# A three-branch decoder layer on one core: an earlier start from the un-normalised input, a hoisted merge gate, and the next block's rows moved

## The chip, the cores and the metric

The kernel runs on one core of a Trainium2 chip, on core 0. The metric is the device time of one execution in microseconds: 2474.88 us, median of 3 runs (2473.91 to 2475.95).

## What is computed

One layer reads x (2048 tokens of 1024 channels), normalises each token, projects it by one large matrix, sends the columns of the projection through three token mixers, weights each mixer's lifted output by a gate, sums, projects and adds to x. Cut to its main lines:

```python
h = _rmsnorm(x, norm_w[l])
proj = h @ w_in[l]
(a_q, a_f, a_i, a_g, b_qkv, b_z, b_beta, b_a,
 c_q, c_k, c_v, c_g, gate_logits) = jnp.split(proj, split_points, axis=-1)
y_a = _hgrn2_branch(a_q, a_f, a_i, a_g, lb_all[l], norm_a[l])       # A: gated recurrence, 4 heads
y_b = _gated_deltanet_branch(b_qkv, b_z, b_beta, b_a, conv_w[l], ...)  # B: delta rule, 4 heads, chunks of 64
y_c = _swa_sink_branch(c_q, c_k, c_v, c_g, sinks[l], bias_blk)      # C: attention in a window of 128
lifted = jnp.einsum('bsnc,ncd->bsnd', ys, w_branch[l])
gates = jax.nn.sigmoid(gate_logits.reshape(Bn, S, N_BRANCHES, D_MODEL))
merged = jnp.sum(gates * lifted, axis=2)
x = x + merged @ w_out[l]
return _rmsnorm(x, final_norm)
```

The normalisation is `x * rsqrt(mean(x*x) + eps) * w`: a factor for each token and a factor for each channel. In each chunk, branch B inverts a unit triangular 64 x 64 matrix (`triangular_solve`).

## The kernel before, in words

The tokens are worked in four blocks of 512 (`block`, s = 0 to 3). Every float32 product is split: each factor is written as a high and a low part, and three matmuls (high by high, high by low, low by high) stand for one. One weight tile is 128 x 512 for the high and for the low part and serves four steps of 128 channels, so `mm_ct` (L97) issues 12 matmuls for each tile: L102, L103 and L104 are its three matmuls. They write a bank of PSUM with the tag d (ps_d, four banks). The mixers' own small matmuls write the banks c0 and c1 (ps_c, two each).

In block 0 a weight tile comes from DRAM as `wraw`; ACT makes the high part (L87), DVE the low part (L88), and the pair is stored as `kept`. The later blocks load the kept pair into one of four buffers (L83).

The start (L207 to L221): the transposed x, times the channel factor, is split into uH and uL (un-normalised), and the projections of v, beta and the like are taken from u and scaled row by row afterwards. `load_x` (L124) loads one of eight row tiles of x (L127) and squares it on ACT with a running sum (L129); `norm_rows` and `norm_scale` make the factor of each token from these sums, spread it over the partitions by matmuls of diagonals (dg from POOL at L141, matmul L143) and copy it to R (L145). `norm_h` multiplies x by R (L158) and splits into hH (ACT, L107) and hL (DVE, L108). All further projections read h. For the blocks 1 to 3 the eight `load_x`, `norm_rows` and `norm_scale` stand at the end of the block before, in the merge of branch C, and ACT issues their loads.

The merge: `gate(n, dt)` projects one tile of gate logits and takes a tanh on ACT (L360), `lift` projects the branch's output and combines; n is the branch, dt one of eight channel tiles. One gate is 24 matmuls of L102 to L104 on hH and hL, one lift is 12 on yH and yL.

Branch B, a head h: `unit_b(h)` is the first phase. It makes NT (products of keys), copies its 64 x 64 corners to NS on ACT (L581), stores them to a DRAM scratch (L582), loads the 16 x 16 diagonal blocks as L (L585), inverts these on DVE by a loop of pairs L589 and L591, stores, loads the result as XB and transposes it into X (L596). `unit_b2` is the second phase: two levels of matmul L611 (reads X and NS), four copies to yb (L615, two on ACT and two on DVE), matmul L621 and a masked copy into X (L626); then L638 and the rest, and the recurrence over chunks (L655 and after). Branch C, a unit j: `unit_c` makes logits and exponentials E, `unit_c2` transposes E (L750), copies it to PT (ACT, L752) and multiplies it by the values (L759).

The order of the instructions on each engine is fixed when the program is built. The phases are written so that the second phase of one head stands after the first phase of the next (L811 to L861), and a scheduler interleaves them. `tc.issue_after(x)` puts what it encloses behind instruction x: L611 stands behind the last matmul issued by `mm_ct` before it (`last_mm`), so whatever projections are written ahead of the call stand ahead of L611. The lines that set this order around the change are

```python
f3(yA); pb1 = unit_b(1); f0 = pb0(); merge(0, yA, range(2)); f1 = pb1(); merge(0, yA, range(2, KT))
pb2 = unit_b(2); f1(yB); pb3 = unit_b(3); pb2()(yB); c0 = unit_c(0); pb3()(yB); c1 = unit_c(1)
```

"Head one" to "head four" below are h = 0 to 3, and "head one of the recurrence" is `unit_a(0)`.

Of the kernel before, what the change touches and what calls it, by code (L numbers as in the profile page):

```python
# [11 lines left out]
F32 = mybir.dt.float32  # L12
# [3 lines left out]
AF = mybir.ActivationFunctionType  # L16
# [4 lines left out]
P = 128  # L21
# [31 lines left out]
def _trunk(tc, S, a, out):  # L53
# [40 lines left out]
    last_mm, last_act, last_ld, last_dve = [None], [None], [None], [None]  # L94

# [35 lines left out]
    def norm_rows(sq):  # L131
        rs = sb.tile([P, NT], F32, name="rsx", tag="rsx")
        G.tensor_tensor(rs, sq[:, :, 0], sq[:, :, 1], op=ALU.add)
        rsq(rs, rs, 1.0 / D, EPS)
        return rs
# [70 lines left out]
    def start(kt):  # L206
        xT0.append(load_xT(0, kt, SLOT[kt], 2))  # L207
        uH.append(sb.tile([P, TB], F32R, name="uH", tag="msum", bufs=KT + 1))
        split(uH[kt], uL[kt], xT0[kt], normw[:, kt:kt + 1])
        load_x(0, sq0, kt, SLOT[kt])  # L210

    pj0 = mm_tc(a["wtc"][0], NTC, uH, uL, each=start)
    rs0 = norm_rows(sq0)
# [110 lines left out]
    def block(s, hH, hL, last=None):  # L324
        t0 = s * TB

        def proj_ct(idx):
            p = bank()
            mm_ct(p, a["wct"][idx], hH, hL, KT)
            return p  # L330

        def gate_ct(idx):
            pg = proj_ct(idx)
            gt = sb.tile([P, TB], F32, name="gt", tag="gt")
            silu2(gt, pg)
            return gt
# [20 lines left out]
        def gate(n, dt):  # L357
            gp = proj_ct(37 + n * KT + dt)
            th = sb.tile([P, TB], F32, name="gth", tag="gth", bufs=GB)
            A.activation(th, gp, AF.Tanh, scale=0.5)  # L360
            return th
# [22 lines left out]
        def unit_a(h):  # L384
# [4 lines left out]
            pf = proj_ct(4 + h)  # L389
# [5 lines left out]
            pq = proj_ct(h)  # L395
            silu2(Q, pq)
            gt = gate_ct(8 + h)
# [422 lines left out]
        pb1 = unit_b(1)  # L820
        f0 = pb0()
        merge(0, yA, range(2))
# [6 lines left out]
        pb3 = unit_b(3)  # L829
        pb2()(yB)  # L830
# [4 lines left out]
        merge(1, yB, range(2))  # L835
# [9 lines left out]
        c3()(yC)  # L845
        if s + 1 < NSB:
            sq = sb.tile([P, NT, 2], F32, name="sqx", tag="sqx")
            with tc.issue_after(last_act[0]):
                for i in range(2 * NT):
                    load_x(s + 1, sq, i, eng=A)  # L850
            rs = norm_rows(sq)
        for dt in range(3):
            lift(2, dt, g[dt], yC)
        merge(2, yC, range(3, 6))
        if s + 1 < NSB:
            R = norm_scale(rs, last_mm[0])
        merge(2, yC, range(6, KT))
# [97 lines left out]
```

## Time and profile before

| what | value |
| --- | --- |
| device time, median of 3 runs | 2474.88 us |
| the profiled execution, device time | 2470.34 us |
| its span, first to last instruction | 2468.6 us |
| PE (matmul) busy | 2403.5 us, 97% |
| DVE busy | 1168.6 us, 47% |
| ACT busy | 866.2 us, 35% |
| POOL busy | 437.5 us, 18% |

A busy time is the sum over one engine's instructions. Matmuls are pipelined, so one that is listed with 0.39 us lets the next start 0.23 us after its own start. In a timeline row the first number is the start in us from the start of the span, the second the duration (of all its instructions, with a count behind x), and the brackets hold the idle time of that engine just ahead of it and what released it. The granted clock is given in parts of full speed, 2.4 GHz.

### The profile page before, as it was taken

The numbers are of one execution on the slowest core, as the hardware profiler recorded it, in microseconds if no ns is written. First come the engines' busy times: TensorE is split into PE (matmuls) and PEld (weight loads), VectorE is DVE, ScalarE is ACT, GpSimd is POOL, SyncE is SP. The second block draws the span as 40 slices with busy tenths as digits, with TensorE's granted clock in tenths as the row PEclk, the third lists the DMA queues.
The fourth block names the chain that finished last, engine by engine and source line by source line (L and its number), as shares of the span: only waits on it lengthen the run. The fifth ranks groups of instructions, "written<-read, shape, count | busy, mean of one in ns | idle before, by whom it ended". The sixth has DMA issues, their size and how long they took to land. (4 is left out here: it accounts for less than half of the span.)

```text
span 2468.6 us, 37448 instructions
## 1 busy us (share of the span) xinstructions
PE 2403.5 (97%) x13658; PEld 1930.1 (78%) x13658; DVE 1168.6 (47%) x3188; ACT 866.2 (35%) x2285; POOL 437.5 (18%) x821
## 2 busy tenths in 40 slices
PE   7999999999999999999999999999999999999998
PEld 7777777878877777787887868778788786877886
DVE  5667477455245626613324562652232465274311
ACT  5455355354334313414223521341322342233211
POOL 3322021112122101111112210111111221011011
PEclk9999999999999999999999999999999999999999
DMA  6756673878844445355774445435666453543564
GB/s 226 244 195 230 225 256 123 282 248 318 289 135 125 143 165 159 106 179 194 240 215 129 139 137 175 150 105 188 208 214 207 129 157 119 183 143 117 168 202 170
DMA packets 193156, 452.84 MB, mean 183 GB/s; under 512 B 52243, under 2 KB 70588, under 8 KB 192844
## 3 DMA queue, kind: packets, MB, share of 16 engines
q1 hardware_dynamic: 180812, 442.05, 54.7%
q10 hardware_dynamic: 12160, 8.39, 1.1%
q8 instruction: 108, 1.77, 0.3%
q14 instruction: 76, 0.62, 0.1%
HBM read 348.81 MB, written 103.14 MB: 183 GB/s over the span
## 5 line engine op out<-in xcount | busy, mean ns | idle before, releaser
L102 PE MATMUL ps_d<-hH,wHL 128*128 128x512 f32 x1952 | 785.0, 402 | 7.7 <-ACT hH L107 5.6
L103 PE MATMUL ps_d<-hL,wHL 128*128 128x512 f32 x1952 | 781.3, 400 | 1.3 <-DVE hL L108 1.3
L104 PE MATMUL ps_d<-hH,wHL 128*128 128x512 f32 x1952 | 779.3, 399 | 0.0
L102 PEld LDWEIGHTS ps_d<-hH,wHL 128*128 128x128 f32 x1952 | 369.0, 189 | 76.9 <-ACT hH L107 5.7
L103 PEld LDWEIGHTS ps_d<-hL,wHL 128*128 128x128 f32 x1952 | 368.7, 189 | 71.8 <-issue 2.2
L104 PEld LDWEIGHTS ps_d<-hH,wHL 128*128 128x128 f32 x1952 | 368.3, 189 | 70.4 <-issue 1.8
L88 DVE TENSOR_TENSOR wHL<-wraw,wHL 128x512 fp32r<-128x512 f32 (+1 forms) x194 | 130.0, 675 | 115.8 <-ACT wHL L87 110.8
L374 POOL TENSOR_TENSOR msum<-msum,gth 128x512 f32<-128x512 f32 x64 | 90.0, 1408 | 407.5 <-DVE gth L373 387.6
L87 ACT CAST wHL<-wraw 128x512 fp32r<-128x512 f32 (+1 forms) x194 | 113.7, 592 | 134.2 <-PE ps_d L104 87.9
L360 ACT ACTIVATE gth<-ps_d 128x512 f32<-128x512 f32 x96 | 57.4, 598 | 289.3 <-PE ps_d L104 288.2
L103 PE MATMUL ps_d<-yL,wHL 128*128 128x512 f32 x384 | 153.7, 402 | 0.0
L102 PE MATMUL ps_d<-yH,wHL 128*128 128x512 f32 x384 | 153.5, 401 | 0.0
L104 PE MATMUL ps_d<-yH,wHL 128*128 128x512 f32 x384 | 152.9, 400 | 0.0
L373 DVE SCALAR_TENSOR_TENSOR gth<-gth,ps_d 128x512 f32<-128x512 f32 x64 | 43.9, 687 | 203.9 <-PE ps_d L104 203.9
L174 PE MATMUL ps_d<-wHL,mH 128*128 128x512 f32 x256 | 99.5, 390 | 2.7 <-DMA wHL<-kept 2.7
L175 PE MATMUL ps_d<-wHL,mH 128*128 128x512 f32 x256 | 99.6, 389 | 0.0
L176 PE MATMUL ps_d<-wHL,mL 128*128 128x512 f32 x256 | 99.5, 389 | 0.0
L517 DVE SCALAR_TENSOR_TENSOR qkB<-raw,convw,qkB 128x512 f32<-128x512 f32 x96 | 71.7, 747 | 44.1 <-ACT qkB L515 42.7
L121 ACT ACTIVATE th<-ps_d 128x512 f32<-128x512 f32 x64 | 38.3, 598 | 130.2 <-PE ps_d L104 120.8
L103 PEld LDWEIGHTS ps_d<-yL,wHL 128*128 128x128 f32 x384 | 72.4, 188 | 14.6 <-issue 1.2
L102 PEld LDWEIGHTS ps_d<-yH,wHL 128*128 128x128 f32 x384 | 72.2, 188 | 14.7 <-issue 0.7
L104 PEld LDWEIGHTS ps_d<-yH,wHL 128*128 128x128 f32 x384 | 72.4, 189 | 14.1 <-issue 1.2
(280 smaller groups left out, 3758.7 us busy)
## 6 DMA issues: line engine op xcount, KB each, us to landing
wHL<-kept SPq DMA_DIRECT2D x486, 512.0 KB, 3.5
kept<-wHL SPq DMA_DIRECT2D x162, 512.0 KB, 4.0
wraw<-in_wct_dram SPq DMA_DIRECT2D x122, 256.0 KB, 3.5
wHL<-kept SPq DMA_DIRECT2D x32, 324.0 KB, 3.7
xT<-in_xT_dram SPq DMA_DIRECT2D x32, 256.0 KB, 4.8
rt<-in_x_dram SPq DMA_DIRECT2D x32, 256.0 KB, 3.9
out_dram<-rt SPq DMA_DIRECT2D x32, 256.0 KB, 3.9
wraw<-in_wb_dram SPq DMA_DIRECT2D x24, 256.0 KB, 3.8
```

What stands on the lines that cost most here:

```text
L87: A.copy(w[:, 0, :n], raw[:, :n])
L88: V.tensor_tensor(w[:, 1, :n], raw[:, :n], w[:, 0, :n].bitcast(F32), op=ALU.subtract)
L102: T.matmul(p, wh[:, ks], rh[kt], start=(kt == 0), stop=False)
L103: T.matmul(p, wh[:, ks], rl[kt], start=False, stop=False)
L104: last_mm[0] = T.matmul(p, wl[:, ks], rh[kt], start=False, stop=(kt == nk - 1)).ins
L174: T.matmul(pj[j][:, :n], lh[kt][:, js], wh, start=(kt == 0), stop=False)
L175: T.matmul(pj[j][:, :n], lh[kt][:, js], wl, start=False, stop=False)
L176: last = T.matmul(pj[j][:, :n], ll[kt][:, js], wh, start=False, stop=(kt == KT - 1)).ins
L360: A.activation(th, gp, AF.Tanh, scale=0.5)
L373: last_dve[0] = V.scalar_tensor_tensor(th, th, 1.0, lp, op0=ALU.add, op1=ALU.mult).ins
L374: G.tensor_tensor(m, m, th, op=ALU.add)
L517: V.scalar_tensor_tensor(dst, raw[:, j:j + TB], convw[:, ti, j:j + 1], dst, op0=ALU.mult, op1=ALU.add)
```

## The change

It has four parts. (1) At the start, `load_x` lags two channel tiles behind the split of u. (2) In block 0, head one of the recurrence takes its three projections from u (`raw`) and DVE multiplies each by R into a new tile `scaled`. (3) In each block the first gate of the merge of branch A is written ahead of head one's second phase, `pb0()`, and the first gate of the merge of branch B ahead of head three's, `pb2()`; their lifts stay where they were. (4) The next block's `load_x` calls move from behind unit C's last phase into the merge of branch C, behind its fourth lift and behind the fourth gate's tanh; the `norm_scale` moves one merge step later.

```diff
@@ -92,6 +92,7 @@
         return w[:, 0, :n], w[:, 1, :n]
 
     last_mm, last_act, last_ld, last_dve = [None], [None], [None], [None]
+    last_tanh = [None]
 
     def mm_ct(p, src, rh, rl, nk):
         for q in range(nk // 4):
@@ -207,9 +208,12 @@
         xT0.append(load_xT(0, kt, SLOT[kt], 2))
         uH.append(sb.tile([P, TB], F32R, name="uH", tag="msum", bufs=KT + 1))
         split(uH[kt], uL[kt], xT0[kt], normw[:, kt:kt + 1])
-        load_x(0, sq0, kt, SLOT[kt])
+        if kt > 1:
+            load_x(0, sq0, kt - 2, SLOT[kt - 2])
 
     pj0 = mm_tc(a["wtc"][0], NTC, uH, uL, each=start)
+    for i in (KT - 2, KT - 1):
+        load_x(0, sq0, i, SLOT[i])
     rs0 = norm_rows(sq0)
     marks = []
     pj1 = mm_tc(a["wtc"][1], NTC, uH, uL, tags=("d", "d", "c1", "c1"), marks=marks)
@@ -324,13 +328,18 @@
     def block(s, hH, hL, last=None):
         t0 = s * TB
 
-        def proj_ct(idx):
+        def proj_ct(idx, raw=False):
             p = bank()
-            mm_ct(p, a["wct"][idx], hH, hL, KT)
-            return p
-
-        def gate_ct(idx):
-            pg = proj_ct(idx)
+            if not raw:
+                mm_ct(p, a["wct"][idx], hH, hL, KT)
+                return p
+            mm_ct(p, a["wct"][idx], uH, uL, KT)
+            t = sb.tile([P, TB], F32, name="scaled", tag="gth", bufs=GB)
+            V.tensor_tensor(t, p, R0, op=ALU.mult)
+            return t
+
+        def gate_ct(idx, raw=False):
+            pg = proj_ct(idx, raw)
             gt = sb.tile([P, TB], F32, name="gt", tag="gt")
             silu2(gt, pg)
             return gt
@@ -357,7 +366,7 @@
         def gate(n, dt):
             gp = proj_ct(37 + n * KT + dt)
             th = sb.tile([P, TB], F32, name="gth", tag="gth", bufs=GB)
-            A.activation(th, gp, AF.Tanh, scale=0.5)
+            last_tanh[0] = A.activation(th, gp, AF.Tanh, scale=0.5).ins
             return th
 
         def lift(n, dt, th, yT):
@@ -386,15 +395,16 @@
             hs = slice(h * P, (h + 1) * P)
             qk = sb.tile([P, 2, TB], F32, name="qk", tag="qk")
             Q, K = qk[:, 0, :], qk[:, 1, :]
-            pf = proj_ct(4 + h)
+            raw = s == 0 and h == 0
+            pf = proj_ct(4 + h, raw)
             F = sb.tile([P, TB], F32, name="F", tag="w0")
             A.activation(F, pf, AF.Sigmoid)
             A.activation(K, pf, AF.Sigmoid, scale=-1.0)
             A.activation(F, F, AF.Identity, scale=omlb[:, h:h + 1], bias=lb[:, h:h + 1])
             A.activation(K, K, AF.Copy, scale=omlb[:, h:h + 1])
-            pq = proj_ct(h)
+            pq = proj_ct(h, raw)
             silu2(Q, pq)
-            gt = gate_ct(8 + h)
+            gt = gate_ct(8 + h, raw)
             prod = sb.tile([P, TB], F32, name="prod", tag="w1")
             G.tensor_tensor(prod, Q, K, op=ALU.mult)
             V.tensor_tensor(Q, Q, F, op=ALU.mult)
@@ -818,8 +828,10 @@
         pb0 = unit_b(0)
         f3(yA)
         pb1 = unit_b(1)
+        g = gate(0, 0)
         f0 = pb0()
-        merge(0, yA, range(2))
+        lift(0, 0, g, yA)
+        merge(0, yA, range(1, 2))
         f1 = pb1()
         merge(0, yA, range(2, KT))
         yB = new_y()
@@ -827,12 +839,14 @@
         pb2 = unit_b(2)
         f1(yB)
         pb3 = unit_b(3)
+        g = gate(1, 0)
         pb2()(yB)
         c0 = unit_c(0)
         pb3()(yB)
         c1 = unit_c(1)
         f0 = c0()
-        merge(1, yB, range(2))
+        lift(1, 0, g, yB)
+        merge(1, yB, range(1, 2))
         f1 = c1()
         merge(1, yB, range(2, KT))
         yC = new_y()
@@ -843,18 +857,19 @@
         c2()(yC)
         g = [gate(2, dt) for dt in range(3)]
         c3()(yC)
+        for dt in range(3):
+            lift(2, dt, g[dt], yC)
+        merge(2, yC, range(3, 4))
         if s + 1 < NSB:
             sq = sb.tile([P, NT, 2], F32, name="sqx", tag="sqx")
-            with tc.issue_after(last_act[0]):
+            with tc.issue_after(last_tanh[0]):
                 for i in range(2 * NT):
                     load_x(s + 1, sq, i, eng=A)
             rs = norm_rows(sq)
-        for dt in range(3):
-            lift(2, dt, g[dt], yC)
-        merge(2, yC, range(3, 6))
+        merge(2, yC, range(4, 7))
         if s + 1 < NSB:
             R = norm_scale(rs, last_mm[0])
-        merge(2, yC, range(6, KT))
+        merge(2, yC, range(7, KT))
         if s + 1 < NSB:
             with tc.issue_after(last_dve[0]):
                 hs = norm_h(R, lambda kt: load_xT(s + 1, kt))
```

The places where this moves instructions follow, as the program's order has them. The changed file's line numbers are higher: L102 to L108 and L127 to L158 by one, L360 and L370 by nine, L589 to L638 and L752 by ten. L338 is the new product `scaled`.

The first place is DVE at the start of block 0. Before, the last rows ahead of the normalisation and the rows up to the first work behind it:

```order
L198 TENSOR_SCALAR ba<-ps_c_297,rsx 128x8
L88 TENSOR_TENSOR wHL<-wraw,wHL 128x512
L158 TENSOR_TENSOR xT<-xT,R 128x512 x2
L108 SCALAR_TENSOR_TENSOR hL<-xT,normw,hH 128x512 x4
L158 TENSOR_TENSOR xT<-xT,R 128x512
L108 SCALAR_TENSOR_TENSOR hL<-xT,normw,hH 128x512
L158 TENSOR_TENSOR xT<-xT,R 128x512
L108 SCALAR_TENSOR_TENSOR hL<-xT,normw,hH 128x512 x3
L88 TENSOR_TENSOR wHL<-wraw,wHL 128x512
L481 TENSOR_TENSOR xa<-ba,dtb 128x16
L482 SCALAR_TENSOR_TENSOR ab<-xa 128x16
```

and now:

```order
L199 TENSOR_SCALAR ba<-ps_c_297,rsx 128x8
L159 TENSOR_TENSOR xT<-xT,R 128x512 x2
L109 SCALAR_TENSOR_TENSOR hL<-xT,normw,hH 128x512 x4
L159 TENSOR_TENSOR xT<-xT,R 128x512
L109 SCALAR_TENSOR_TENSOR hL<-xT,normw,hH 128x512
L159 TENSOR_TENSOR xT<-xT,R 128x512
L109 SCALAR_TENSOR_TENSOR hL<-xT,normw,hH 128x512 x3
L338 TENSOR_TENSOR scaled<-ps_d,R 128x512
L88 TENSOR_TENSOR wHL<-wraw,wHL 128x512 x4
L491 TENSOR_TENSOR xa<-ba,dtb 128x16
L492 SCALAR_TENSOR_TENSOR ab<-xa 128x16
```

Before, one L88 stands ahead of the normalisation (L158 and L108) and one behind it; now none of this stretch stands ahead, and the first `scaled` and four L88 stand behind it.

The second place is head one of block 1. On PE the second phase of a delta-rule head begins with L611. Before, from the last matmul of the keys' products (L562):

```order
L562 MATMUL ps_c_8416<-qkB 128x256 x2
L562 MATMUL ps_c_8423<-qkB 128x256 x2
L103 MATMUL ps_d<-hL,wHL 128x512
L104 MATMUL ps_d<-hH,wHL 128x512
L102 MATMUL ps_d<-hH,wHL 128x512
L103 MATMUL ps_d<-hL,wHL 128x512
L104 MATMUL ps_d<-hH,wHL 128x512
L611 MATMUL ps_c_8477<-X,NS 64x64 x4
L102 MATMUL ps_d<-hH,wHL 128x512
L103 MATMUL ps_d<-hL,wHL 128x512
L104 MATMUL ps_d<-hH,wHL 128x512
L102 MATMUL ps_d<-hH,wHL 128x512
```

and now the end of the stretch between the same two lines, which are L572 and L621 there:

```order
L105 MATMUL ps_d<-hH,wHL 128x512
L103 MATMUL ps_d<-hH,wHL 128x512
L104 MATMUL ps_d<-hL,wHL 128x512
L105 MATMUL ps_d<-hH,wHL 128x512
L103 MATMUL ps_d<-hH,wHL 128x512
L104 MATMUL ps_d<-hL,wHL 128x512
L105 MATMUL ps_d<-hH,wHL 128x512
L621 MATMUL ps_c_8514<-X,NS 64x64 x4
L103 MATMUL ps_d<-yH,wHL 128x512
L104 MATMUL ps_d<-yL,wHL 128x512
L105 MATMUL ps_d<-yH,wHL 128x512
L103 MATMUL ps_d<-yH,wHL 128x512
```

Before, five matmuls of `mm_ct` stand between the two lines; now 17 do, the same kind, and the lift on yH, which stood later, follows L621 at once. On DVE, the end of the same head's two levels and the start of head two's inversion (L589), before:

```order
L615 COPY yb_506<-ps_c_8477 64x2x32 x2
L626 COPY_PREDICATED X<-bmask,ps_c_8486 64x2x2x16 x4
L632 STREAM_TRANSPOSE XB<-X 64x256 x2
L615 COPY yb_506<-ps_c_8497 64x2x32 x2
L626 COPY_PREDICATED X<-bmask,ps_c_8506 64x2x32 x4
L635 STREAM_TRANSPOSE XB<-X 32x4x32 x2
L589 TENSOR_TENSOR L16t<-L_8440 32x14
L592 MEMSET L_8440 32x16
L643 COPY Y_8524<-ps_c_8517 64x256
L591 TENSOR_TENSOR L_8440<-L_8440,L16t 32x14
```

and now:

```order
L625 COPY yb_506<-ps_c_8514 64x2x32 x2
L636 COPY_PREDICATED X<-bmask,ps_c_8523 64x2x2x16 x4
L642 STREAM_TRANSPOSE XB<-X 64x256 x2
L625 COPY yb_506<-ps_c_8534 64x2x32 x2
L379 SCALAR_TENSOR_TENSOR msum<-gth,ps_d 128x512
L599 TENSOR_TENSOR L16t<-L_8446 32x14
L602 MEMSET L_8446 32x16
L636 COPY_PREDICATED X<-bmask,ps_c_8543 64x2x32
L601 TENSOR_TENSOR L_8446<-L_8446,L16t 32x14
L636 COPY_PREDICATED X<-bmask,ps_c_8543 64x2x32
L599 TENSOR_TENSOR L16t<-L_8446 32x26
L636 COPY_PREDICATED X<-bmask,ps_c_8543 64x2x32
```

The first L599 (L589 before), which reads head two's L, has moved ahead of the four masked copies L636 (L626 before) of head one's second level, and the following pairs alternate with them.

The third place is ACT at the end of block 1, around the last copies of unit C to PT. Before:

```order
L129 ACTIVATE scrp,sqx<-xs 128x512
L127 DMA xs<-in_x_dram 128x512
L360 ACTIVATE gth<-ps_d 128x512
L129 ACTIVATE scrp,sqx<-xs 128x512
L127 DMA xs<-in_x_dram 128x512
L129 ACTIVATE scrp,sqx<-xs 128x512 x2
L360 ACTIVATE gth<-ps_d 128x512
L752 COPY PT<-ps_c_11112 128x512
L752 COPY PT<-ps_c_11119 128x512
L752 COPY PT<-ps_c_11136 128x512
L752 COPY PT<-ps_c_11143 128x512
L107 ACTIVATE yH<-gt 128x512
```

and now:

```order
L762 COPY PT<-ps_c_11118 128x512
L762 COPY PT<-ps_c_11125 128x512
L762 COPY PT<-ps_c_11142 128x512
L762 COPY PT<-ps_c_11149 128x512
L108 ACTIVATE yH<-gt 128x512
L108 ACTIVATE mH<-msum 128x512 x3
L369 ACTIVATE gth<-ps_d 128x512
L128 DMA xs<-in_x_dram 128x512 x2
L130 ACTIVATE scrp,sqx<-xs 128x512
L128 DMA xs<-in_x_dram 128x512
L108 ACTIVATE mH<-msum 128x512
```

Before, the loads (L127) and squares (L129) stand ahead of the four copies to PT, between the gates' tanh; now the four copies come first, then the splits of m (L108), the fourth gate's tanh (L369), and the loads and squares behind it, with splits between.

## Rows read from the trace of the kernel before

**Rows 1.** The page, parts 1 and 5: PE, and the merge's additions.

```profile
PE 2403.5 (97%) x13658; PEld 1930.1 (78%) x13658; DVE 1168.6 (47%) x3188; ACT 866.2 (35%) x2285; POOL 437.5 (18%) x821
...
L374 POOL TENSOR_TENSOR msum<-msum,gth 128x512 f32<-128x512 f32 x64 | 90.0, 1408 | 407.5 <-DVE gth L373 387.6
```

**Rows 2.** Waits of PE: engine, line, releaser; us in total, times, longest.

```profile
PE ps_c L611 <- DVE X L596: 14.7, 9, 2.8
PE ps_c L759 <- ACT PT L752: 7.2, 6, 2.4
```

**Rows 3.** Timeline of PE, start: start, duration, instruction, count, idle before.

```profile
6.82 0.64 PE L174 MATMUL ps_d<-wHL,uH 128*128 128x324 f32 x1 [6.82 <-ACT wHL L87]
...
39.49 0.85 PE L143 MATMUL ps_c<-dg,onesP 128*128 128x128 f32 x4 [0.32 <-POOL dg L141]
45.90 0.80 PE L102 MATMUL ps_d<-hH,wHL 128*128 128x512 f32 x1 [5.56 <-ACT hH L107]
...
66.97 0.66 PE L417 MATMUL ps_c<-qk 128*64 128x32 f32 x16
```

**Rows 4.** Stretches: us, busy (x) PE, PEld, DVE, ACT, POOL; clock; DMA, GB/s.

```profile
40.30:53.70 13.40, 6.53 (x15) 4.63 (x15) 11.61 (x13) 6.16 (x10) 8.29 (x8) 0.62 0.58 223
53.70:66.90 13.20, 13.20 (x59) 10.70 (x57) 4.93 (x9) 6.94 (x11) 4.56 (x8) 1.00 0.58 208
832.00:835.40 3.40, 3.40 (x9) 2.25 (x10) 1.24 (x6) 1.22 (x4) 0.00 (x0) 0.51 0.16 41
1146.10:1149.40 3.30, 3.30 (x22) 2.79 (x23) 0.43 (x1) 0.62 (x2) 1.59 (x4) 0.50 0.02 7
1440.40:1443.80 3.40, 3.40 (x21) 2.55 (x22) 1.70 (x7) 1.23 (x4) 0.13 (x1) 1.00 0.11 34
```

**Rows 5.** Timeline of DVE, start of block 0.

```profile
41.00 2.36 DVE L158 TENSOR_TENSOR xT<-xT,R 128x512 f32<-128x512 f32 x2 [0.51 <-ACT R L145]
...
50.83 2.07 DVE L108 SCALAR_TENSOR_TENSOR hL<-xT,normw,hH 128x512 fp32r<-128x512 f32 x3
54.23 0.69 DVE L88 TENSOR_TENSOR wHL<-wraw,wHL 128x512 fp32r<-128x512 f32 x1 [1.34 <-ACT wHL L87]
```

**Rows 6.** Timeline of PE, delta-rule head one of block 1.

```profile
831.52 0.45 PE L611 MATMUL ps_c<-X,NS 128*64 128x64 f32 x8 [2.83 <-DVE X L596]
...
842.45 0.33 PE L638 MATMUL ps_c<-X,NTt 64*64 64x64 f32 x2
```

**Rows 7.** Same place, timelines of ACT, SP and DVE; and DMA issues.

```profile
834.31 0.21 ACT L615 COPY yb<-ps_c 64x64 f32<-64x64 f32 x1 [0.91 <-ACT NS L581]
...
837.33 0.38 SPq L585 DMA_DIRECT2D L<-scrN  x1
...
843.58 0.16 DVE L589 TENSOR_TENSOR L16t<-L 32x14 f32<-32x14 f32 x1
...
L<-scrN SPq DMA_DIRECT2D x16, 32.0 KB, 3.2
```

**Rows 8.** Timeline of PE at three other heads' first L611.

```profile
972.13 0.45 PE L611 MATMUL ps_c<-X,NS 128*64 128x64 f32 x8 [1.53 <-DVE X L596]
...
1440.39 0.45 PE L611 MATMUL ps_c<-X,NS 128*64 128x64 f32 x8 [2.38 <-DVE X L596]
...
1470.94 0.45 PE L611 MATMUL ps_c<-X,NS 128*64 128x64 f32 x8 [1.15 <-DVE X L596]
```

**Rows 9.** Timelines of ACT and PE, end of block 1; line L127's loads.

```profile
1142.73 0.63 ACT L129 ACTIVATE scrp<-xs 128x512 bf16<-128x512 f32 x1 [3.64 <-DMA xs<-in_x_dram]
...
1146.03 1.97 PE L759 MATMUL ps_c<-PT,cv__74 128*64 128x128 f32 x16 [2.42 <-ACT PT L752]
...
DMA to landing us min/median/max: 2.5/4.6/6.0
```

**Rows 10.** Timelines of ACT and PE, merge of branch C, block 1.

```profile
1164.75 0.60 ACT L360 ACTIVATE gth<-ps_d 128x512 f32<-128x512 f32 x1 [0.91 <-PE ps_d L104]
...
1183.59 0.60 PE L143 MATMUL ps_c<-dg,onesP 128*128 128x128 f32 x4
```

## The prediction

> **What bounds the kernel now.** I read the page first: the matrix engine PE is busy 2403.5 us of a span of 2468.6 [rows 1], so only some 65 us can be had without taking matmuls away, and the change takes none away. The question is which of PE's waits go, and which come. The table of waits names them: 14.7 us in nine waits before L611 (the first matmul of a delta-rule head's second phase, which needs X from DVE) and 7.2 us in six waits before L759 (which needs PT from ACT) [rows 2]. The timeline of the first 67 us shows two more: 6.82 us until the first matmul, and 5.56 us before the first projection of normalised h [rows 3]. The stretches show a cost that no wait shows: after some of them PE runs at half clock. From 40.3 to 53.7 us it is busy 6.53 of 13.40 us at a clock of 0.62; for 3.4 us after 832.0 and after 1146.1 the clock is 0.51 and 0.50, so each of these loses some 1.7 us; after 1440.4 it stays 1.00 [rows 4]. Off these places PE runs 59 matmuls in 13.2 us [rows 4], 0.224 us each. That is the price of all filler below: 12 matmuls (one weight tile) are 2.7 us.
>
> **The change, part by part.** No matmul is added. DVE gets three products of 128x512 (`scaled`, 0.7 us each); they stand beside PE.
>
> *A, the start.* The first square leaves ACT's queue ahead of the first weight cast, which PE's first matmul at 6.82 waits for [rows 3]: some 0.5 us. Then head one of the recurrence in block 0 reads the un-normalised u, so PE need not wait for h at 45.90. Its 72 matmuls end in the row of before where L417 starts, 66.97 [rows 3]. If nothing held them they would take 72 x 0.224 = 16.1 us from about 38.5 (39.49 less its wait of 0.32 and the 0.6 of diagonals ahead of it), so until 54.6. Something does hold them: in the new order the fourth weight tile's low half (L88) and the first `scaled` stand on DVE behind the whole normalisation (first place of the order). That ran from 41.00 to 50.83 + 2.07 = 52.90 [rows 5]. The diagonals of the row scale are now made early, before PE's wait at 39.49 [rows 3], so I let it start 1.2 us sooner and end at 51.7; one `scaled` and one L88 (0.69 [rows 5]) later it is 53.1. By then PE has 40 of the 72 done (24 + 12 that have both halves, and the high halves of two more tiles), having stood about 5 us. The other 32 take 7.2 us, so head one ends at 60.3 at full clock, 6.7 us sooner. If these stands bring a half-clock stretch as the old one did, 7.2 becomes up to 10.8 and the gain 3.1. I take 4.5, between the two. Bounds: 0.5 (PE stands as long as before) and 12.4 (nothing holds).
>
> The Trainium skill ("TensorE: Matmul & The Clock Gate", Part 1) says that the throttled clock is the default, that activity releases it, and that the monitor runs free of the program; the trace agrees, since 2.83 us of waiting brought half clock in one block and 2.38 us brought none in the next [rows 4, 6, 8]. By that rule A is either 3.1 or 6.7, and the sum below 1.4 lower or 2.2 higher.
>
> *B, heads one of blocks 1 to 3.* Before, 12 of the gate's matmuls stood ahead of L611; L611 must follow the last matmul issued, so now all 24 do (second place of the order), and 2.7 us of work covers the waits of 2.83 and 2.38 [rows 6, 8] and the third like it. With the half clock after two of them that is 7.6 + 3.4 = 11 us at most. Part is given back in the same head. (1) L621 needs the second copy of yb, which ACT makes at 834.31, behind the scratch stores [rows 7]; PE now reaches it with 6 matmuls after L611 at full clock, at 833.3, so 1.4 us are lost. (2) On DVE, L589 of the next head now stands before this head's last L626 (second place; it ran behind them at 843.58 [rows 7]). L589 needs L, whose load is issued at 837.33 and lands 3.2 us later [rows 7], at 840.5. L626 is held until then, and L638, which PE would reach at 840.6, starts near 841.8: 1.2 us and some tenths. In block 1 the comparison point is L638 at 842.45 [rows 6]: 0.6 us sooner with six more matmuls done is 2.0 us. The same working gives 1.8 in block 2 and 2.1 in block 3, and 0.3 more for head two of block 2, whose X comes sooner because L589 does. B is 6.2; its bounds are -2 (the waits come back in full, with L589 held longer) and 11.
>
> *C, heads three of blocks 1 to 3.* The same gate ahead of a wait of 1.53 us [rows 8] and two of about that size, 4.9 us in all. The 12 extra matmuls push L611 itself 1.2 us later than it was, and with it ACT's copy and the stores; I leave 1.1 of each, so 3.3. Bounds 0 and 4.9. In block 0 the order of heads one to three does not move.
>
> *D, the next block's rows.* Before, the eight loads and squares stand on ACT between the gates and PT (third place of the order): a square waits 3.64 us for its load at 1142.73, and PE waits 2.42 us for PT behind it, with half clock after it [rows 4, 9]. Of the 7.2 us of rows 2 some 6.7 lie there (block 3, without loads, has next to none); with 1.7 for the clock, 8.4 go. What is late next: the loads now start after the tanh of the fourth gate of the merge (1164.75 + 0.6) and must be done before the diagonal matmuls, which move by one merge step, 36 x 0.224 = 8.1 us, from 1183.59 to 1191.7 [rows 10]. That leaves 26.4 us. Two buffers hold the rows, a load takes 4.6 us (2.5 to 6.0 [rows 9]) and a square with its read 0.8, so four pairs take about 25 us with ACT's splits between, and the scale and its first diagonals 2 us more: PE waits some 0.7 us. The second pair of diagonals then stands on POOL behind a merge addition, 1.4 us [rows 1]. I take 2 us for each of blocks 1 and 2. In block 0 ACT also casts the weights, and one cast now stands behind the fifth square, about 17.5 us after the first load, while PE wants it after six tiles, 16.3 us: with its low half and what follows, 3 us. 8.4 - 7 = 1.4; bounds -17 and 8.4.
>
> **Sum.** 4.5 + 6.2 + 3.3 + 1.4 = 15.4. Head four's second phase is reordered against unit C's logits in every block, in rows I cannot price; I take 2 off for it: 13.4. The profiled execution took 2470.34 us, so 2456.9; the median of the timed runs, 2474.88, lies 4.5 higher, so it becomes 2461.5.
>
> **Rivals.**
> - *The waits only move.* X of head two is made by a chain on DVE and DMA that does not ask where PE is; a PE that no longer waits at head one waits at head two. For it: in block 2 head two's X came 1.15 us after PE, at 1470.94 [rows 8]. Against it: L589, which stood 3 us past its data, moves forward. B, C and D are then 0 and A 3: 2471.9, no change.
> - *All waits stay away.* A 6.7, B 11, C 4.9, D 8.4: 31 us, 2444. Against it: the order on DVE and ACT above.
> - *Slower: the rows come late.* If a load takes 6.1 us and more, near the top of rows 9, instead of 4.6, four pairs take 28 us, PE stands 5 us before the diagonals in each of three blocks and runs at half clock after it (1.7), and in block 0 the casts cost 5 more: D is -17, the sum with the other terms and the 2 taken off is -5.0, 2479.9; beyond 6.5 us a load it is 2485. For it: the square at 1142.73 waited 3.64 us with nothing else on ACT [rows 9]. Against: the median. Below some 5.8 us it doesn't decide.
>
> **How the numbers follow.** Forecast 0.60, alone 2456 to 2467; waits move 0.21; all away 0.12; slower 0.07. What a measurement of this kernel can tell from no change is about 0.2%, 5 us: faster is below 2469.9, slower above 2479.8. The forecast and the second rival are faster whole, and a third of the first rival: 0.60 + 0.12 + 0.07 = 0.79. Two thirds of the first rival but a hundredth are the same, 0.14 with rounding; the rest, 0.07, is slower. The range runs from 2451, short of most of the second rival, to 2473, past the middle of the first; the slower one lies outside.
>
> **What would show it.** A right: L417 of block 0 starts at 60 to 64 us, and PE stands near 47 to 53 us for DVE's L88 and ACT's casts. B and C right: X is no releaser of PE in heads one and three, but L626 waits for the load of L and PE stands for yb and L638. D right: PT releases nothing of PE, and POOL's dg does, for 1 to 3 us in each of three blocks. The forecast is wrong if L611 of head two gathers waits of 2 us and more, if dg costs over 5 us a block, or if PE's waits in head four's second phase grow past 2 us a block.

## The result, and the profile after

The changed kernel takes 2463.11 us (median of 5 runs, 2457.43 to 2465.59), the kernel before 2474.88: ratio 0.9944, 95% interval 0.9931 to 0.9958. The forecast was 2461.5 with a range of 2451 to 2473. Measured again beside the experiments, the changed kernel gave 0.9963 (0.9947 to 0.9979). The profiled execution took 2457.43 us, the fastest of its five, with a span of 2455.6 us; it is 12.9 us below the profiled one of before.

The page's first part after, against [rows 1]:

```profile
PE 2405.0 (98%) x13658; PEld 1929.3 (79%) x13658; DVE 1169.4 (48%) x3191; ACT 863.4 (35%) x2285; POOL 436.1 (18%) x821
```

PE's idle time (span less busy) went from 65.1 to 50.6 us. The table of PE's waits (engine, line, releaser: us in total, times, longest), against [rows 2]:

```profile
PE ps_c L621 <- DVE QKT L577: 5.1, 6, 1.5
PE ps_d L103 <- ACT wHL L87: 4.4, 3, 2.4
PE ps_c L621 <- DVE X L606: 3.9, 6, 1.1
PE ps_c L631 <- DVE yb L625: 2.3, 7, 0.4
PE ps_c L144 <- POOL dg L142: 1.6, 2, 1.2
```

L621 is L611 of before. X releases it for 3.9 us where it was 14.7; but 5.1 us now end with L577, a product on DVE that reads the same c bank of PSUM and comes last of the head's first phase. The waits for PT are gone from the top of the table; casts (L87) and the diagonals' dg stand there instead.

Where the time went is read at places where PE has done the same work in both kernels: the first matmul of each block's recurrence (L417, now L427), the eighth lift of branch A and of branch B (the products L370 and L373, now L379 and L382), and PE's last matmul. Each entry is the gain of that stretch, in us, from the starts in the two timelines:

| block | to L417/L427 | from there to the 8th lift of A (heads one, two) | to the 8th lift of B (heads three, four) | to the next block's L417/L427, or the end |
| --- | --- | --- | --- | --- |
| 0 | 0.73 | -0.53 | -0.08 | -3.57 |
| 1 | | 3.97 | 1.42 | 2.57 |
| 2 | | 1.37 | 1.37 | 1.29 |
| 3 | | 1.94 | 1.76 | 0.67 |

They sum to 12.9. The -3.57 is clock, not a wait: PE sits idle for 5.9 us in that stretch, where it was 6.8. Stretches after (us, busy and count of PE, PEld, DVE, ACT, POOL; clock; DMA share, GB/s):

```profile
54.70:61.50 6.80, 5.86 (x14) 4.15 (x14) 4.51 (x9) 3.44 (x5) 3.19 (x9) 0.50 0.65 215
638.40:641.80 3.40, 3.40 (x15) 3.40 (x14) 0.53 (x2) 0.00 (x0) 0.61 (x2) 0.50 0.88 268
665.80:669.20 3.40, 3.40 (x10) 2.63 (x9) 0.00 (x0) 0.00 (x0) 0.00 (x0) 0.51 0.98 396
```

and the last two places in the kernel before:

```profile
638.10:641.50 3.40, 3.40 (x25) 3.40 (x24) 0.55 (x3) 0.46 (x1) 0.61 (x2) 1.00 0.85 263
663.00:666.40 3.40, 3.40 (x15) 2.82 (x16) 0.00 (x0) 0.00 (x0) 0.00 (x0) 1.00 1.03 414
```

The waits ahead of the second place are these, before and after:

```profile
662.99 0.50 PE L102 MATMUL ps_d<-hH,wHL 128*128 128x512 f32 x1 [2.11 <-DMA wHL<-kept]
```

```profile
664.85 0.50 PE L103 MATMUL ps_d<-hH,wHL 128*128 128x512 f32 x1 [2.15 <-DMA wHL<-kept]
```

The same load, 2.11 and 2.15 us, and full clock behind the one, half clock behind the other. That agrees with what the Trainium skill says of the monitor ("TensorE: Matmul & The Clock Gate", Part 1), that it runs free of the program. So one execution's clock is partly luck. The profiles of five later runs say the same of this place: e1, e3, e4, e6 and e9 each have a half-clock stretch that begins between 663 and 666 us, and e1 and e6 leave the rows where the kernel before has them. So it was the profiled execution of before that had luck here. It had bad luck elsewhere: its half-clock stretch at 832 us follows 2.83 us of waiting at head one [rows 4, 6], and in e1, which leaves that head as it was, the same wait (L620 there) is followed by full clock:

```profile
832.87 0.45 PE L620 MATMUL ps_c<-X,NS 128*64 128x64 f32 x8 [2.84 <-DVE X L605]
```

```profile
833.00:836.40 3.40, 3.40 (x22) 2.47 (x22) 1.58 (x7) 1.23 (x4) 0.01 (x1) 1.00 0.10 25
```

In e9, the changed kernel once more, the stretch at 638 us does not return and the one at 666 us does; the same table for its profile sums to 12.2.

### The profile page after: what moved, and what is told of

Its sections match the earlier page's. It is cut to its first block, busy times and chain, and to the rows that moved or that the text cites. A ratio compares the mean times of both kernels' runs of the same rounds, so it can differ in the third digit from the quotient of the medians.

```text
span 2455.6 us, 37449 instructions
## 1 busy us (share of the span) xinstructions
PE 2405.0 (98%) x13658; PEld 1929.3 (79%) x13658; DVE 1169.4 (48%) x3191; ACT 863.4 (35%) x2285; POOL 436.1 (18%) x821
## 5 line engine op out<-in xcount | busy, mean ns | idle before, releaser
L103 PE MATMUL ps_d<-hH,wHL 128*128 128x512 f32 x1928 | 776.2, 403 | 4.5 <-ACT wHL L87 2.4
L104 PE MATMUL ps_d<-hL,wHL 128*128 128x512 f32 x1928 | 770.1, 399 | 0.0
L105 PE MATMUL ps_d<-hH,wHL 128*128 128x512 f32 x1928 | 766.9, 398 | 0.0
L103 PEld LDWEIGHTS ps_d<-hH,wHL 128*128 128x128 f32 x1928 | 363.7, 189 | 74.0 <-ACT wHL L87 2.8
L105 PEld LDWEIGHTS ps_d<-hH,wHL 128*128 128x128 f32 x1928 | 362.9, 188 | 70.8 <-issue 0.9
L104 PEld LDWEIGHTS ps_d<-hL,wHL 128*128 128x128 f32 x1928 | 363.6, 189 | 66.9 <-issue 1.5
L88 DVE TENSOR_TENSOR wHL<-wraw,wHL 128x512 fp32r<-128x512 f32 (+1 forms) x194 | 129.3, 673 | 109.5 <-ACT wHL L87 108.9
L369 ACT ACTIVATE gth<-ps_d 128x512 f32<-128x512 f32 x96 | 57.3, 597 | 293.6 <-PE ps_d L105 285.3
L87 ACT CAST wHL<-wraw 128x512 fp32r<-128x512 f32 (+1 forms) x194 | 113.6, 591 | 121.4 <-PE ps_d L105 75.0
L382 DVE SCALAR_TENSOR_TENSOR gth<-gth,ps_d 128x512 f32<-128x512 f32 x64 | 43.8, 685 | 190.7 <-PE ps_d L105 175.6
L105 PEld LDWEIGHTS ps_d<-yH,wHL 128*128 128x128 f32 x384 | 72.3, 188 | 15.6 <-issue 2.1
```

The source lines that it names most:

```text
L87: A.copy(w[:, 0, :n], raw[:, :n])
L88: V.tensor_tensor(w[:, 1, :n], raw[:, :n], w[:, 0, :n].bitcast(F32), op=ALU.subtract)
L103: T.matmul(p, wh[:, ks], rh[kt], start=(kt == 0), stop=False)
L104: T.matmul(p, wh[:, ks], rl[kt], start=False, stop=False)
L105: last_mm[0] = T.matmul(p, wl[:, ks], rh[kt], start=False, stop=(kt == nk - 1)).ins
L369: last_tanh[0] = A.activation(th, gp, AF.Tanh, scale=0.5).ins
```

## The experiments

All ratios are against the kernel before on the same chip; "clock" is the mean granted clock over a kernel's runs, "idle" span less PE's busy time in the profile. The kernel before has clock 0.9925 beside e1 to e8, 0.9926 beside e9 to e11 and 0.9936 beside e12, and idle 65.1.

| kernel | median us | ratio (95%) | clock | idle us |
| --- | --- | --- | --- | --- |
| e1 start alone | 2477.52 | 1.0000 (0.9987 to 1.0013) | 0.9928 | 65.2 |
| e2 both gates alone | 2461.54 | 0.9937 (0.9921 to 0.9953) | 0.9950 | 56.5 |
| e3 rows alone | 2476.84 | 0.9996 (0.9978 to 1.0015) | 0.9930 | 64.4 |
| e4 changed, late normalisation | 2464.39 | 0.9949 (0.9932 to 0.9965) | 0.9953 | 55.2 |
| e5 gate one alone | 2471.61 | 0.9981 (0.9969 to 0.9993) | 0.9941 | 62.0 |
| e6 gate three alone | 2475.23 | 0.9986 (0.9967 to 1.0005) | 0.9915 | 61.3 |
| e7 gates, rows spread | 2454.93 | 0.9910 (0.9891 to 0.9930) | 0.9963 | 53.8 |
| e8 e7 and more gates | 2462.41 | 0.9945 (0.9924 to 0.9966) | 0.9925 | 50.3 |
| e9 the changed kernel | 2466.10 | 0.9963 (0.9947 to 0.9979) | 0.9944 | 51.9 |
| e10 e7 and unit C's gates | 2452.36 | 0.9912 (0.9894 to 0.9930) | 0.9965 | 48.6 |
| e11 e7 and the start | 2457.03 | 0.9929 (0.9911 to 0.9947) | 0.9958 | 50.3 |
| e12 e10 and a mended start | 2451.41 | 0.9923 (0.9902 to 0.9944) | 0.9973 | 43.4 |

**e1.** The start alone: of the change's diff, the lag of `load_x` and the `raw` projections.

> Only the start is changed (the lag of the row loads and the raw first head of the recurrence in block 0); the gates and the next block's rows stay as before. The prediction gave this part 4.5 us (bounds 0.5 and 12.4). Theory from the two traces: the normalisation holds DVE until some 55 us, the fourth weight tile's low half waits behind it, and a half-clock stretch follows; L427 of block 0 (L417 before, at 66.97) starts at 65.5 to 66.8, the second head's at 92 to 93, and the time is 0 to 2 us below the kernel before. Rival, that the forecast was right and only the profiled execution of the changed kernel shows less: L427 at 60 to 64 and 3 to 6 us.

The ratio is 1.0000, so a gain of 4.5 us lies outside (3.2 us either way). In the profile the first recurrence starts at 65.84, within the theory's 65.5 to 66.8 and off the rival's 60 to 64, and PE's idle time is the same. The start is worth next to nothing.

**e2.** The gates alone.

```diff
+        g = gate(0, 0)
         f0 = pb0()
-        merge(0, yA, range(2))
+        lift(0, 0, g, yA)
+        merge(0, yA, range(1, 2))
...
+        g = gate(1, 0)
         pb2()(yB)
...
```

> Only the two hoisted gates are in. The prediction gave heads one 6.2 us and heads three 3.3 us, less 2 for head four: 7.5. Theory from the two traces, read at the lifts of each block: heads one 1.4 to 4.0 us in each of blocks 1 to 3 (7.3 together), heads three 1.4 to 1.8 in each (4.5 together), nothing in block 0: 11 to 12 us in a profile where the two kernels have the same half-clock stretches elsewhere, and 7 to 12 in the medians. Rival (the waits only move): 0 to 2 us, with X as releaser of 2 us and more at heads two and four.

15.6 us by the ratio (11.6 to 19.6), over the 7 to 12 expected for the medians. PE's idle fell by 8.6 us; the mean clock rose from 0.9925 to 0.9950, and 0.0025 of 2475 us is 6.2 us more, by this estimate 14.8 together. PE's waits that stay:

```profile
PE ps_c L759 <- ACT PT L752: 7.4, 4, 3.4
PE ps_c L611 <- DVE QKT L567: 4.9, 6, 1.5
PE ps_c L611 <- DVE X L596: 4.0, 7, 0.9
```

**e3.** The rows alone: `load_x` behind the fourth gate's tanh, the scale one merge step later.

> Only the next block's row loads, squares and scale are moved into the last merge. The prediction gave this 1.4 us: 8.4 taken from the waits before L759 and 7 given back before the diagonals' matmuls. Theory from the two traces: the waits before L759 go (6.7 us and one half-clock stretch), the diagonals cost 0.4 us in all, a late weight cast 1.4 us in block 0: 4 to 6 us faster. Rival (rows come late): slower by 5 us, with waits of 3 us and more before L144.

0.9996 is 1.0 us (-3.7 to 5.5): the forecast's 1.4 fits, the theory's 4 to 6 us lies at the edge, and the rival's loss of 5 us lies outside. Its profile shows both halves. Read at the first lift of branch C in blocks 0 to 2 (the stretch of the waits before L759), PE gains 2.58, 3.59 and 0.91 us, 7.1 together. From there to that merge's last lift it loses 2.7, 5.1 and 0.5. The middle one is a late row: the last square waits for its load and runs at 1192.26 us, and the factor and dg follow it. The timeline of PE, and the stretch after it:

```profile
1195.19 0.84 PE L144 MATMUL ps_c<-dg,onesP 128*128 128x128 f32 x4 [2.43 <-POOL dg L142]
```

```profile
1197.30:1200.70 3.40, 3.40 (x11) 2.82 (x12) 1.29 (x2) 1.76 (x4) 1.41 (x2) 0.51 0.03 13
```

**e4.** The changed kernel with the normalisation behind the raw head.

```diff
-    hs_ = norm_h(R0, lambda kt: xT0[kt], (V, G))
+    hs_ = (None, None)
...
         f0 = unit_a(0)
         if s == 0:
+            hH, hL = norm_h(R0, lambda kt: xT0[kt], (V, G))
             bias_rows()
```

> The changed kernel with the normalisation of block 0 written behind the raw first head instead of ahead of it, so that the fourth weight tile's low half and the first scaled product stand on DVE among the products of the normalisation and not behind them. Theory (DVE's order holds the start): L427 of block 0, at 66.24 in the changed kernel, starts at 58 to 62, PE's stands at 50 to 56 us shrink to under 2 us. What is left of it at the end of block 0: by the same theory 4 to 8 us and a time of 2455 to 2460. Rival (the chain of the inverse through DRAM sets head one in block 0 and takes it back): L427 early, but head one's L621 waits longer by as much, and the time equals the changed kernel's within 2 us. Second rival: PE stands for h instead, and L427 is at 64 or later.

The theory's 58 to 62 us for L427 and its 2455 to 2460 us are both missed. PE's stands at 50 to 56 us are gone, and a third wait stands in their place; here it is on PE, and then the row of DVE that ends it:

```profile
63.20 1.07 PE L427 MATMUL ps_c<-qk 128*64 128x32 f32 x16 [4.89 <-DVE qk L410]
```

```profile
62.36 0.69 DVE L410 TENSOR_TENSOR qk<-qk,F 128x512 f32<-128x512 f32 x1 [2.08 <-POOL prod L409]
```

L427 needs L410's product. L410 overwrites q and so waits for POOL's L409, which reads q and starts only at 61.06 us, behind six products of the same head (L450, 3.67 us). So the last 2.1 us of this wait are POOL's queue, not DVE's. The ratio, 0.9949, lies between the changed kernel's two, 0.9944 and 0.9963.

**e5 and e6.** One hoisted gate each.

> Only the gate ahead of head one's second phase is hoisted. Theory (both hoists work by the wait of their own head, and the times add): 6 to 10 us below the kernel before; waits of 1.5, 1.9 and 1.5 us stay at heads three (972, 1581 and 2188 us in the kernel before). Rival (one hoist does all, since it shifts what follows): 12 us and more, with heads three's waits gone as well. Second rival (the wait moves): X releases heads two and three later, by 1 us and more each, and the time is 3 us or less below.

> Only the gate ahead of head three's second phase is hoisted. Theory: 4 to 7 us below the kernel before, by heads three alone; heads one keep waits of 2.3 to 2.9 us and the half-clock stretch after some of them. Rival: 0 to 2 us, since head four's X comes late instead.

4.7 us (1.7 to 7.7) and 3.5 (-1.2 to 8.2), both a little under the 6 to 10 and the 4 to 7 expected; e6 alone is not clear of no change. PE's idle falls by 3.1 and 3.8, which add to 6.9 of e2's 8.6. X's share of L611's waits in e5 and in e6:

```profile
PE ps_c L611 <- DVE X L596: 8.6, 6, 2.4
```

```profile
PE ps_c L611 <- DVE X L596: 9.9, 8, 2.8
```

Each hoist takes X's waits at its own heads, as the theory had it. But in e5 part of what is taken at heads one comes back at heads three, which X now holds for 2.43 us in each of the three blocks, the first of them shown here:

```profile
974.02 0.45 PE L611 MATMUL ps_c<-X,NS 128*64 128x64 f32 x8 [2.43 <-DVE X L596]
```

That is 7.3 us, where these waits are 4.9 us in the kernel before and 5.4 and 5.7 in e1 and e3, which leave these heads alone; and half clock follows two of the three. So with one gate the rival "the waits only move" is right in part. The times add to 8.2 of 15.6, but the intervals are too wide to call the two more than additive.

**e7.** The gates, and the rows in the merge of branch B, SP issuing their loads.

```diff
...
+        for dt in range(3, KT):
+            merge(1, yB, range(dt, dt + 1))
+            if s + 1 < NSB and dt < 7:
+                with tc.issue_after(last_tanh[0]):
+                    for i in (2 * dt - 6, 2 * dt - 5):
+                        load_x(s + 1, sq, i)
...
```

> The two hoisted gates, and the next block's row loads and squares spread over the merge of branch B, a pair behind the tanh of each of four gates, the loads issued by SP; the scale stays where it was in the kernel before. Theory (the rows cost only where ACT's square stands ahead of PT or where the load is late): the waits before L759, 7.4 us in four with the gates alone, fall under 1 us, no wait before the diagonals comes, and the time is 5 to 9 us below the gates alone (2461.54): 2453 to 2457. Rival (ACT has no room in that merge, or the loads hold SP's weights): waits before L102 for kept weights or for ACT's casts in block 0 grow by 3 us and more, and the time is that of the gates alone.

2454.93 us, as the theory said. No wait for PT stands in the table of PE's waits any more, and for dg there is one of 0.3 us, the start's, which the kernel before has too. Against e2 that is 6.7 us by the two ratios, whose intervals just overlap: the rows are probably worth some us once they are put where ACT has room.

**e8.** e7, with a second gate ahead of heads one and of unit C's transposes, and in both places a third between the two phases that follow.

```diff
-        g = gate(0, 0)
+        g = [gate(0, 0), gate(0, 1)]
         f0 = pb0()
...
+        g = [g, gate(1, 1)]
         f0 = c0()
...
```

> As e7_gates_spread, and each of the two stretches has one gate more: a second one ahead of head one's second phase, a second one ahead of unit C's first transposes (L750), and a third written between the phases that follow, so that their cover stays. Theory (each wait is worth itself): heads one lose another 4 us of waits before L611, L750 its 4.3 us; 2444 to 2451. Rival (what ends these waits is DVE's queue, which is as long as before, and the cover taken from the later phases comes back as waits there): within 2 us of e7_gates_spread.

7.5 us slower than e7, though PE idles 3.5 us less. The timelines of PE and DVE at head one of block 2, and the stretch behind:

```profile
1442.30 0.47 PE L622 MATMUL ps_c<-yb,XB 128*64 128x64 f32 x2 [2.46 <-DVE yb L616]
```

```profile
1440.33 0.16 DVE L590 TENSOR_TENSOR L16t<-L 32x14 f32<-32x14 f32 x1 [6.93 <-DMA L<-scrN]
...
1442.02 0.22 DVE L616 COPY yb<-ps_c 64x64 f32<-64x64 f32 x1
```

```profile
1442.30:1452.30 10.00, 10.00 (x33) 6.04 (x33) 5.29 (x24) 0.62 (x3) 0.00 (x0) 0.50 0.17 59
```

At heads one and three of blocks 1 to 3 the first matmul (L611, here L612) no longer waits; but on DVE the next head's L590 (L589 before) now stands ahead of the copy of yb, and L590 waits 6.93 us for its load. PE waits 2.46 us for yb, and 10 us at half clock follow. Over the whole profile yb costs 9.8 us, and half clock lasts 10.2 us here and 13.7 us from 1582 us on, behind another wait for yb. e10 has the same edit in unit C without the one at heads one: there yb costs 2.4 us and neither half-clock stretch comes. So it is the edit at heads one that spoils e8. This is the mechanism that the prediction had put a price on one step later, at L626.

**e9.** The changed kernel once more.

> The changed kernel itself, on the chip and beside the runs of the next two. Theory (the gates give all of the gain, the start and the rows nothing): its time is the gates' alone, 0.993 to 0.995 of the kernel before. Rival (start and rows give their 5.9 us and the first measurement missed it): 0.990 to 0.992.

0.9963 is above the 0.993 to 0.995 of the theory and far from the rival's 0.990 to 0.992: start and rows add nothing to the gates that can be seen. Whether they cost something is not shown, since the interval overlaps that of e2.

**e10 to e12.** e10 is e7 with e8's second edit alone (unit C); e11 is e7 with the change's start; e12 is e10 with the start and the diagonals behind the last un-normalised projection.

```diff
-    R0 = norm_scale(rs0, marks[2 * NT - 1])
+    R0 = norm_scale(rs0, marks[-1])
```

> The gates and the spread rows (e7), and only in unit C one gate more: gate (1, 1) ahead of the first transposes L750 and gate (1, 2) between the two phases; head one keeps one gate. Theory (each wait is worth itself, and what spoilt e8 was DVE at heads one): the 4.3 us before L750 go, nothing comes back: 2449 to 2453. Rival (the order that the scheduler makes elsewhere shifts as in e8): yb waits at L621 of 1 us and more, and 2456 or above.

> The gates and the spread rows (e7), with the changed start added. Theory (the start gives nothing, as in e1): 2453 to 2457, within 2 us of e7. Rival (the start gives its forecast 4.5 us once the rest is out of its way): 2449 to 2452.

> The kernel of e10 (gates, spread rows, unit C's extra gates) with the changed start, in which the diagonals of the row scale are issued behind the last matmul of the un-normalised projections (as the kernel before has them) and not in the middle, where the changed kernel has PE wait 1.24 us for them and end these projections at 41.23 instead of 38.41. Theory (the lost 2.8 us come from that place, and the rest of the start is held by the normalisation on DVE): these projections end at 38 to 39, L427 starts at 63 to 65 instead of 66.24, and the time is 1 to 4 us below e10 (2452.36): 2448 to 2451. Rival (what the start gains, DVE and the load of the inverse take back before head one's L621): L427 early as above, but the time within 1.5 us of e10. Second rival (the half clock follows the stands wherever they are): L427 at 66 again.

e10's time is within the 2449 to 2453 expected. The waits before unit C's transposes in e7 and in e10:

```profile
PE ps_c L751 <- DVE E L738: 4.3, 4, 1.7
```

```profile
PE ps_c L751 <- DVE E L738: 1.3, 1, 1.3
```

So 3.0 of the 4.3 us go; but the ratio is that of e7 (0.9912 and 0.9910), so a gain over e7 is not shown. On one chip e10 took 2452.36 us and the changed kernel 2466.10. e11 took 2457.03 us, 2 us more than e7 on another chip, and the start's forecast is missed again. In e12 the theory's first step fails: the un-normalised projections end at 41.99 us, not at 38 to 39, since PE meets late casts instead of the late diagonals. L427 starts at 65.16 us, neither at the 63 to 65 of the theory and the first rival nor at the second rival's 66, and the time is 1 us below e10's on another chip, the ratio 0.0011 above. So the mended start, too, adds nothing that can be seen.

```profile
32.98 0.41 PE L175 MATMUL ps_d<-wHL,uH 128*128 128x324 f32 x1 [1.59 <-ACT wHL L87]
...
65.16 0.66 PE L427 MATMUL ps_c<-qk 128*64 128x32 f32 x16
```

So e7 and e10 beat both kernels; e12 beats the kernel before and the second measurement of the changed one, and its interval overlaps that of the first. Among the three the runs do not decide.

## Why the prediction was right, and where it was not

The time came out as forecast, the direction too; the terms did not all.

**A, the start, forecast 4.5: wrong.** L427 comes 0.7 us sooner in the profile and 0.1 us later in e9's, and e1 and e11 show no gain in time. The first small part came true: PE's first matmul starts at 6.19 us, 0.6 sooner. The step that failed is "I let it start 1.2 us sooner": the normalisation began at 43.03 instead of 41.00, two later. PE at the start:

```profile
26.85 0.41 PE L175 MATMUL ps_c<-wHL,uH 128*128 128x324 f32 x1 [0.80 <-ACT wHL L87]
...
29.62 0.73 PE L144 MATMUL ps_c<-dg,onesP 128*128 128x128 f32 x3 [1.24 <-POOL dg L142]
...
41.38 0.60 PE L144 MATMUL ps_c<-dg,onesP 128*128 128x128 f32 x4
...
54.42 0.56 PE L103 MATMUL ps_d<-hH,wHL 128*128 128x512 f32 x1 [2.38 <-ACT wHL L87]
...
56.34 0.80 PE L105 MATMUL ps_d<-uH,wHL 128*128 128x512 f32 x1 [0.94 <-DVE wHL L88]
...
66.24 0.66 PE L427 MATMUL ps_c<-qk 128*64 128x32 f32 x16
```

and DVE:

```profile
43.03 2.39 DVE L159 TENSOR_TENSOR xT<-xT,R 128x512 f32<-128x512 f32 x2 [0.32 <-ACT R L146]
...
55.01 0.68 DVE L338 TENSOR_TENSOR scaled<-ps_d,R 128x512 f32<-128x512 f32 x1
55.61 2.48 DVE L88 TENSOR_TENSOR wHL<-wraw,wHL 128x512 fp32r<-128x512 f32 x4
```

The diagonals come in two pairs, and R needs both. Only the first pair was moved forward, into the middle of the second un-normalised projection. The second still stands behind the last un-normalised matmul, as before (L144 at 41.38), and so it is in e1, e9 and e11: the normalisation could not begin before that matmul. And that matmul starts at 41.23 instead of 38.41 us. Compared matmul by matmul, PE is 1.1 us ahead of before until 26 us. It then loses 1.5 us at a cast, and 2.1 us around the first pair of diagonals, of which 1.24 us is waiting for dg and 0.6 us the pair's own matmuls, with 0.3 us more shortly after.

The wait for dg has this cause. POOL before and after (L402 and L412 are one memset, for a tile of head one; L117 and L118 the power that makes the row factor, from which dg is made):

```profile
21.69 1.16 POOL L117 TENSOR_TENSOR rsx<-rsx,mhalf 128x4 f32<-128x4 f32 x1
...
29.96 0.31 POOL L402 MEMSET ST<- 64x256 f32 x1 [6.03 <-DMA scrX<-zb]
```

```profile
22.39 0.20 POOL L134 TENSOR_TENSOR rsx<-sqx 128x4 f32<-128x4 f32 x1 [0.48 <-ACT scrp L130]
...
27.20 0.31 POOL L412 MEMSET ST<- 64x256 f32 x1 [4.61 <-DMA scrX<-zb]
...
28.00 1.08 POOL L118 TENSOR_TENSOR rsx<-rsx,mhalf 128x4 f32<-128x4 f32 x1
```

Before, the factor was done ahead of that memset, which by the profile waits for a store (scrX). Now the memset stands between the sum of the squares (L134) and the power, and the factor is done at 29.08 us instead of 22.85. I named POOL's queue for the merge and not here. The same three POOL rows, at the same times within 1 us, are in e1 and e12; that moving the memset would mend it was not tried. The cast's loss has another cause, its load, and so have the four copies on ACT that read the factor (L192, at 25.92 before):

```profile
26.33 0.46 ACT L87 CAST wHL<-wraw 128x324 fp32r<-128x324 f32 x1 [3.01 <-DMA wraw<-in_wtc_dram]
...
30.33 0.21 ACT L276 ACTIVATE nea<-nea 128x4 f32<-128x4 f32 x1 [0.50 <-DMA nea<-in_alog_dram]
30.44 1.78 ACT L192 ACTIVATE vA<-ps_d,rsx 128x324 f32<-128x324 f32 x4
```

They stand behind L276, which waits for a load until 30.33 us, 1.2 us after the factor is there; so in this order the memset explains the late diagonals and not the late copies. In this profile PE does not wait for the casts behind those copies; in e12 it does.

What follows is as forecast: PE stands for the cast and for L88, and a half-clock stretch of 6.8 us comes. Of the two values that the forecast stood between, the one with half clock is 3.1; less the 3.2 us that lie between 1.2 sooner and 2.0 later, nothing is left of it. In block 0 all but 0.2 of the 0.7 us is gone at head one, whose X came no sooner from its load:

```profile
222.09 0.45 PE L621 MATMUL ps_c<-X,NS 128*64 128x64 f32 x8 [1.10 <-DVE X L606]
```

**B, heads one, forecast 6.2: right in size**, 7.3 in blocks 1 to 3 of the profile, two half-clock stretches of before in it (3.4 us); what I had given back was not lost. Head one of block 1 on PE and DVE, against [rows 6, 7]:

```profile
834.72 0.45 PE L621 MATMUL ps_c<-X,NS 128*64 128x64 f32 x8 [0.69 <-DVE QKT L577]
...
837.08 0.33 PE L631 MATMUL ps_c<-yb,XB 128*64 128x64 f32 x2 [0.32 <-DVE yb L625]
...
843.19 0.33 PE L648 MATMUL ps_c<-X,NTt 64*64 64x64 f32 x2
```

```profile
841.61 0.15 DVE L599 TENSOR_TENSOR L16t<-L 32x14 f32<-32x14 f32 x1
...
842.40 0.22 DVE L636 COPY_PREDICATED X<-bmask,ps_c 64x64 f32<-64x64 uint8 x1 [0.59 <-PE ps_c L631]
```

The wait of 2.83 is 0.69 and ends with DVE's last product, not with X; yb costs 0.32 where I had 1.4. L636 stands behind L599 as forecast, but the load had landed: L636 waits for PE. L648 starts 0.74 us later than before, in a block whose L427 came 3.46 us later: 2.7 sooner, where I had 0.6. At heads two, where the first rival expected the waits, PE does not wait for X in blocks 1 to 3.

**C, heads three, forecast 3.3, and 2 taken off for head four: mis-sized together.** 1.3 was forecast for both; the profile has 1.42, 1.37 and 1.76, 4.6, and 4.2 in e9's. At heads three X's waits of 4.9 us are gone, and 1.6 us for L577 and 1.0 for yb are left. At heads four X does hold PE now, 0.5 us in each of the three blocks, one of them here:

```profile
1603.46 0.45 PE L621 MATMUL ps_c<-X,NS 128*64 128x64 f32 x8 [0.52 <-DVE X L606]
```

But a wait of 0.86 us for the transposes of head three's output, which stood just ahead in each block before (L348), is gone, and I had not seen that one. So head four lost nothing in sum, and the 2 us were taken off for a loss that did not come.

**D, the rows, forecast 1.4: borne out, as far as can be told.** The last column of the first table, block 3 left out, sums to 0.3 with the 3.4 us of the two half-clock stretches in it; e3 measured 1.0 (-3.7 to 5.5), 7.1 taken and 8.3 given back in its profile, where I had 8.4 and 7. In the changed kernel's profile, read at the same places, 7.1 is taken and only 2.7 given back by the merge's last lift. So the give-back changes from run to run with the landing of the loads: in block 1 PE waits 2.43 us at one dg in e3 and not at all in the changed kernel. The sign that I named, 1 to 3 us of dg in each of three blocks, did not come there: 0.3 us in one.

So 13.4 came out as 12.9 in the profiles, 11.8 by the medians and 9.2 by the ratio of e9. That it came so near is luck: two errors went against each other, the start 4 too high, heads one to four 4 too low, and the profile's clock was part of it. The gates carry all of it (e2), and about 6 of their 15 us is clock by the estimate above. I had priced the clock only at the places where one profile showed it. The rival "the waits only move" is refuted for the two gates of the change; it is right in part for gate one alone (e5) and for a second gate at heads one (e8).

## What to carry to other kernels

Before an instruction is moved for PE's sake, check that all that its reader needs moves with it (here one of two pairs of diagonals stayed behind), and read what now stands ahead of its inputs on every engine, POOL too (here a memset waiting for a store held the first pair). Cover a wait with about as much PE work as the wait is long; with more, look first at the next engine in the chain, which may take its transfer's wait in front of this head's copies, as DVE did in e8. A wait costs PE itself and, at a chance, a stretch at half clock behind it, so small waits taken away in many places can gain more than their sum (15.6 us against 8.6 of idle time in e2), and one profile can't price it.

## What the runs showed of the hardware

The granted clock of one unchanged kernel on one core went from 0.990 to 0.994 over 23 runs, and its time from 2466.8 to 2486.3 us. A straight line through these runs has 3.1 us for each 0.001 of clock, of which an estimated 2.5 is the clock itself (0.001 of 2475). In e12 a half-clock stretch of 3.4 us began at 33.9, behind the wait of 1.59 us shown above; in the kernel before 2.38 us of waiting brought none [rows 8], and 2.83 us brought one in the kernel before and 2.84 us at the same place none in e1. The length of one wait does not say whether the clock falls behind it.
